# Rows of the later experts brought by indirect DMA and turned, in place of one-hot products

## The chip, the cores and the metric

The kernel runs on one core of a Trainium2 chip. The metric is the device time of one execution in microseconds (us), as the median of several runs. Engines are named as in the profile: PE is TensorE, PEld its weight load, DVE is VectorE, ACT is ScalarE, POOL is GpSimd, SP is SyncE, which issues most of the DMAs.

## What is computed

A trunk of two layers on 256 tokens of 1024 channels, all in float32. The first layer is attention of two kinds and a dense feed-forward; the second is banded attention and an expert feed-forward. Only the last of these is touched by the change. Cut to what matters:

```python
def moe_swiglu(h, w_router, we_gate, we_up, we_down):      # h is x after its RMS norm
    t = h.reshape(b * s, d)                                # 256 x 1024
    logits = (t @ w_router).astype(F32)                    # 8 experts
    top_val, top_idx = lax.top_k(logits, TOP_K)            # 2 a token
    gates = jax.nn.softmax(top_val, axis=-1)
    combine = jnp.einsum('tk,tke->te', gates, jax.nn.one_hot(top_idx, N_EXPERTS, dtype=F32))
    y = jnp.zeros_like(t)
    for e in range(N_EXPERTS):                             # each 1024 -> 3584 -> 1024
        y = y + combine[:, e:e + 1].astype(t.dtype) * swiglu(t, we_gate[e], we_up[e], we_down[e])
    return y.reshape(b, s, d)
```

The weights of the eight experts are 352 MB (8 x 3 x 1024 x 3584 x 4 bytes), and each is read once.

## The kernel before

The expert stage begins at about 430 us of the profiled span and lasts to its end. The kernel computes an expert only for the tokens that chose it. It gives each expert 96 slots (`CAP`), 64 of them main slots and 32 overflow slots; the overflow products stand in a branch (`arm`, L1118) that runs only if the expert has more than 64 tokens. A later pass for experts with more than 96 tokens (L1426) stands behind another branch.

**Slots.** The router's choice gives for each token and expert `sel` (1 or 0) and `pos` (its slot). `dispatch(e)` (L900) makes on DVE two one-hot matrices of 256 tokens by 96 slots: `dx`, tile `dispx`, whose ones are scaled by the token's reciprocal RMS `rx`, and `dt`, tile `disp`, unscaled. Each takes two DVE instructions (L906), one for each 128 tokens.

**Gather.** `Rows.gather` (L917) multiplies x, token-major in SBUF, with `dx` on PE: for each block of 128 channels two products of 128 tokens. The result is the expert's input, channel-major, in a room `xg` (two rooms, by the expert's parity; one is a part of the tile `oTh`). DVE reads it from PSUM and multiplies it by the norm's gain (L923). This is done twice for an expert, for four channel blocks each.

**Chunks.** The 3584 hidden channels of each expert are cut into chunks, and the experts go in pairs. `order` (L808 on) gives 18 chunks: for experts 0 and 1 five, for 2 and 3 and for 4 and 5 four each (1536 of the even expert, 1536 of the odd one, 2048 even, 2048 odd), for 6 and 7 five. For each chunk `experts` (L1147) does the gate columns, the up columns (`cols`, L1195) and then the down rows of the chunk before (`down`, L1162). `cols` and `down` take weights in batches of up to four pieces: first the main products of the batch, then, in the branch, the overflow products.

**Pieces.** Weights come in pieces of at most 1 MB by SP's queue. `pieces_of` (L843) lists them in the order in which they are consumed, and `Pieces.more` (L858) issues as many as a batch has used. A ring of some twenty buffers (tags `raw`, `rawb`, `w`, `hTl`, and for one use each `yx` and `oTl`) holds them; a DMA waits on SP until the last reader of its buffer is done.

**End of an expert.** After the last up columns of an expert, `turn` (L1038) transposes `dt` of the main slots by products with the identity, and, after the down rows of the chunk before, `turn_over` (L1044) those of the overflow slots. These transposed one-hots later put the expert's output rows back to their tokens (`add`, `add_over`, `finish`).

**Order.** `in_order` (L184) keeps PE, ACT and DVE each in the order of the program text, so a step that waits holds all that is behind it on its engine. In this order, where the next chunk is the first one of an expert, `nxt.room()` makes the two one-hots of that expert right behind `x.turn()`, then come the down rows, `turn_over` and the two gathers:

```python
                nxt = found[to.e] if to and to.i == 0 else None
                if nxt:
                    nxt.room()
                if i:
                    down(i - 1, i)
                if q.last:
                    x.turn_over()
                if nxt:
                    nxt.rows.gather(range(0, 4))
                    nxt.rows.gather(range(4, 8))
```

PSUM has four banks (`spin`, `banks`) in rotation for gate and up columns, gathers, transposes and sums, two for the down sums of the main slots (`za`) and two for those of the overflow slots (`zb`).

Of the kernel before, what the change touches and what calls it, by code (L numbers as in the profile page):

```python
# [47 lines left out]
def kernel(ctx: ExitStack, tc: tile.TileContext, A: dict, out: bass.AP):  # L48
# [772 lines left out]

    def piece():
        return raw_tile().rearrange("p a b -> p (a b)")
# [18 lines left out]

    def pieces_of():  # L843
# [6 lines left out]
        for q, before in zip(chunks, [None] + chunks):  # L850
            for w in (eg[q.e], eu[q.e]):
                for k in range(0, KB, max(1, 2048 // q.n)):
                    yield cols_piece(w, q.c0, q.n, k)
            if before:
                yield from downs(before)
# [19 lines left out]
    with ExitStack() as ph:  # L875
# [6 lines left out]
        both = act.tile([P, 2, P], BF, name="both", tag="disp", bufs=2)  # L882
# [7 lines left out]
        for k in range(GROUPS):  # L890
            nc.gpsimd.memset(quarter[k * OV:(k + 1) * OV, k % 2:k % 2 + 1], 1.0)
        comb = act.tile([P, T, NE], F32, name="comb")
# [7 lines left out]
        def dispatch(e):  # L900

            dt = act.tile([P, T, CAP], F32, name="disp", bufs=2)
            dx = act.tile([P, T, CAP], F32, name="dispx")
            for o, value in ((dx, selx), (dt, sel)):
                for t in range(T):
                    nc.vector.tensor_scalar(o[:, t], slots, pos[:, t, e:e + 1], value[:, t, e:e + 1], op0=OP.is_equal,  # L906
                                            op1=OP.mult)
            return dt, dx

        class Rows:  # L910


            def __init__(self, e, room):
                self.dt, self.dx = dispatch(e)
                self.xg = room

            def gather(self, kbs):  # L917
                o = banks(1)[0].rearrange("p (b s) -> p b s", b=4)
                for b, kb in enumerate(kbs):
                    for t in range(T):  # L920
                        mm(o[:, b, 0:CAP], x[:, t, kb * P:(kb + 1) * P], self.dx[:, t], t == 0, t == T - 1)
                k = kbs[0]
                nc.vector.tensor_tensor(self.xg[:, k:k + 4], o[:, :, 0:CAP],  # L923
                                        cst[:, C_GF1 + k:C_GF1 + k + 4, None].to_broadcast([P, 4, CAP]), op=OP.mult)
# [17 lines left out]
        def main_cols(o, rows, tiles, n, kb0):  # L942

            for b, (c, w) in zip(o, parts(n)):
                for kb, r in enumerate(rows_in(tiles), kb0):
                    for k in range(2):
                        at = k * n // 2 + c
                        mm(b[k * MAIN:(k + 1) * MAIN, 0:w], rows.xg[:, kb, 0:MAIN], r[:, at:at + w],
                           kb == 0, kb == KB - 1)

        def over_cols(o, rows, tiles, n, kb0):
            w = over_width(n)
            for kb, r in enumerate(rows_in(tiles), kb0):
                for k in range(GROUPS):
# [4 lines left out]
                    mm(to, rows.xg[:, kb, MAIN:CAP], cols, kb == 0, kb == KB - 1)  # L959
# [62 lines left out]
        class Expert:  # L1022


            def __init__(self, e, rv):
                self.e, self.rv = e, rv
                self.y, self.yo = ys[e % 2], yos[e % 2]

            def room(self):
                self.rows = Rows(self.e, rooms[self.e % 2])  # L1030

            def turned(self, o, n, ss):

                for t in range(T):
                    for k in range(0, P, n):
                        mm(o[k:k + n, t], self.rows.dt[:, t, ss], ident, True, True)
# [93 lines left out]
        def spans(n):  # L1130

            return [(i, min(4, n - i)) for i in range(0, n, 4)]

# [13 lines left out]
        def experts(rows, feed, first, rvs):  # L1147
# [3 lines left out]
            found[0].rows = rows  # L1151
# [43 lines left out]
            def cols(x, main, over, n, mid=None, end=None):  # L1195
# [3 lines left out]
                for p, (i0, m) in enumerate(cuts):  # L1199
                    tiles = feed.take(m)  # L1200
                    main_cols(main, x.rows, tiles, n, i0 * nk)
# [278 lines left out]
```

## Time and profile before

| | us |
|---|---|
| median of 3 runs (1320.77 to 1322.87) | 1321.46 |
| profiled execution, its own time | 1321.63 |
| span of that execution's instructions | 1319.9 |
| PE busy | 1274.8 |
| DVE busy | 378.9 |
| ACT busy | 322.2 |
| POOL busy | 11.0 |

The profiled execution is one run; its span goes from the first instruction to the end of the last, and 1.7 us of its time lie outside. The granted clock of TensorE was 0.996 over the span. PE's busy time counts matmuls from start to a modelled end, so that products that overlap in the array look like one busy stretch. The stage of the experts is the last two thirds of the span. A group of rows in the timeline has the start, the duration from the first to the last of its instructions, the engine, line, operation, tiles as out<-in, shape, the count, and in brackets the idle time before it and what ended it.

### The profile page before, as it was taken

What the parts mean: (1) busy time and instruction counts of PE and PEld (TensorE: products, weight loads), DVE (VectorE), ACT (ScalarE), POOL (GpSimd) and SP (SyncE); (2) the same over time, 40 slices, a digit from 0 to 9 for tenths busy, and PEclk for the clock granted to TensorE, in tenths of its full rate; (3) what the DMA queues carried; (4) which work ended last, traced back from release to release, by engine and by line L of the source; (5) the groups of instructions that cost most, each with busy time, mean ns of one, the idle gap of its engine ahead of it and who ended that gap; (6) DMA issues with size and microseconds to landing.
All of it is one profiled execution on the core that took longest, in us unless ns stands there. A gap on an engine that the chain in (4) does not pass through costs nothing. (4 is left out here: it accounts for less than half of the span.)

```text
span 1319.9 us, 19560 instructions
## 1 busy us (share of the span) xinstructions
PE 1274.8 (97%) x7887; PEld 698.6 (53%) x7887; DVE 378.9 (29%) x723; ACT 322.2 (24%) x593; POOL 11.0 (1%) x38
## 2 busy tenths in 40 slices
PE   9999999999999989999999999999999999999995
PEld 6777888888777743342444343344433344333442
DVE  7965554446788510000111000111100001110011
ACT  7665544446566400100100000000000010000000
POOL 0000000000000000000000000000000000000000
PEclk9999999999999999999999999999999999999998
DMA  9623555555454989999998999999999999999961
GB/s 348 233 68 127 189 178 175 190 191 182 162 161 148 395 322 404 423 421 420 390 420 368 420 422 424 418 420 409 423 422 421 421 418 422 422 422 419 415 262 38
DMA packets 90254, 426.70 MB, mean 323 GB/s; under 512 B 7568, under 2 KB 10256, under 8 KB 59408
## 3 DMA queue, kind: packets, MB, share of 16 engines
q1 hardware_dynamic: 89056, 422.80, 80.2%
q0 software_dynamic: 640, 2.10, 0.7%
q8 instruction: 85, 1.39, 0.4%
q14 instruction: 41, 0.34, 0.1%
q10 hardware_dynamic: 432, 0.07, 0.0%
HBM read 423.89 MB, written 1.05 MB: 322 GB/s over the span
## 5 line engine op out<-in xcount | busy, mean ns | idle before, releaser
L59 PE MATMUL mm<-w,hTh 128*128 128x512 f32 x736 | 240.1, 400 | 0.4 <-DVE w L143 0.4
L143 DVE TENSOR_TENSOR w<-raw,w 128x1024 fp32r<-128x1024 f32 (+1 forms) x127 | 153.9, 1214 | 90.8 <-ACT w L142 90.4
L59 PEld LDWEIGHTS mm<-w,hTh 128*128 128x128 f32 x736 | 137.7, 188 | 32.5 <-issue 1.3
L142 ACT ACTIVATE w<-raw 128x1024 fp32r<-128x1024 f32 (+1 forms) x127 | 133.5, 1053 | 86.5 <-PE mm L59 51.2
L59 PE MATMUL mm<-w,hTl 128*128 128x512 f32 x368 | 146.5, 398 | 0.0
L1143 DVE TENSOR_TENSOR a<-tr,a 128x512 f32<-128x512 f32 (+1 forms) x16 | 9.7, 609 | 254.7 <-PE tr L59 249.9
L59 PE MATMUL za<-raw,hTh 128*64 128x512 f32 x360 | 81.5, 595 | 0.7 <-PEq L1123 0.7
L59 PEld LDWEIGHTS mm<-w,hTl 128*128 128x128 f32 x368 | 69.4, 188 | 14.8
L1143 DVE TENSOR_TENSOR a<-mm,a 128x512 f32<-128x512 f32 (+1 forms) x16 | 10.3, 642 | 227.7 <-PE mm L59 197.9
L59 PE MATMUL mm<-w,oTh 128*64 128x512 f32 (+2 forms) x224 | 57.3, 522 | 0.9 <-PEq L1123 0.8
L59 PE MATMUL za<-rawb,hTh 128*64 128x512 f32 x256 | 57.6, 593 | 0.4 <-DMA w<-in_od_we_gate 0.2
L59 PE MATMUL mm<-raw,xg 128*64 128x512 f32 (+4 forms) x356 | 56.5, 544 | 0.3 <-PEq L1123 0.3
L59 PE MATMUL tr<-rawb,xg 128*32 128x128 f32 (+4 forms) x484 | 54.9, 450 | 1.8 <-DVEq L1123 1.5
L59 PE MATMUL tr<-raw,xg 128*64 128x512 f32 (+4 forms) x364 | 55.5, 537 | 0.0
L59 PE MATMUL mm<-raw,oTh 128*64 128x512 f32 (+1 forms) x240 | 48.9, 535 | 3.4 <-DVE comb L1399 1.4
L59 PEld LDWEIGHTS za<-raw,hTh 128*64 128x64 f32 x360 | 26.5, 137 | 46.8 <-issue 44.8
L59 PE MATMUL za<-w,hTh 128*64 128x512 f32 x224 | 50.5, 595 | 0.4 <-PEq L1123 0.4
L1145 ACT ACTIVATE a<-mm 128x512 f32<-128x512 f32 (+1 forms) x18 | 10.1, 562 | 161.4 <-PE mm L59 161.3
L59 PE MATMUL mm<-rawb,oTh 128*64 128x512 f32 (+1 forms) x216 | 45.5, 559 | 2.1 <-ACTq L1123 1.2
L59 PE MATMUL tr<-w,xg 128*64 128x512 f32 (+4 forms) x296 | 46.8, 528 | 0.3 <-PEq L1123 0.3
L59 PE MATMUL mm<-rawb,xg 128*64 128x512 f32 (+4 forms) x300 | 46.6, 545 | 0.3 <-DMA w<-in_od_we_down 0.3
L969 ACT ACTIVATE hTh<-tr 128x512 f32<-128x512 f32 (+1 forms) x18 | 9.0, 536 | 149.3 <-PE tr L968 149.3
(340 smaller groups left out, 1466.7 us busy)
## 6 DMA issues: line engine op xcount, KB each, us to landing
raw<-in_od_we_down SPq DMA_DIRECT2D x45, 1024.0 KB, 15.7
rawb<-in_od_we_down SPq DMA_DIRECT2D x32, 1024.0 KB, 15.5
raw<-in_od_we_gate SPq DMA_DIRECT2D x29, 1024.0 KB, 15.4
raw<-in_od_we_up SPq DMA_DIRECT2D x28, 1024.0 KB, 17.8
w<-in_od_we_down SPq DMA_DIRECT2D x28, 1024.0 KB, 16.6
rawb<-in_od_we_up SPq DMA_DIRECT2D x27, 1024.0 KB, 19.4
rawb<-in_od_we_gate SPq DMA_DIRECT2D x23, 1024.0 KB, 14.1
w<-in_od_we_gate SPq DMA_DIRECT2D x20, 1024.0 KB, 15.0
```

The source lines that it names most:

```text
L59: nc.tensor.matmul(o, lhsT, rhs, start=start, stop=stop, skip_group_check=True)
L142: nc.scalar.activation(hi[:, s], r[:, s], AF.Copy)
L143: nc.vector.tensor_tensor(lo[:, s], r[:, s], hi[:, s].bitcast(F32), op=OP.subtract)
L969: nc.scalar.activation(dst[:, b:b + n], pt[:, 0:n], AF.Copy)
L1143: nc.vector.tensor_tensor(a[:, c:c + w], o[:, 0:w], a[:, c:c + w], op=OP.mult)
L1145: nc.scalar.activation(a[:, c:c + w], o[:, 0:w], AF.Silu)
```

## The change

For experts 2 to 7 the one-hot gather goes. Instead:

- `store` writes x (1 MB), when its last residual is added, to a memory tensor `stored`, by two DMAs of SP's queue. They are issued behind the first two pieces that wait for a buffer and ahead of those of the `w`, `hTl` and `yx` buffers.
- `lists_in`, behind the up columns of chunk 1, makes the unscaled one-hots of experts 2 to 7 (12 instructions of DVE, into the tile `oTl`), multiplies them on PE with a two-column table `token` (token number and `rx`), and copies the result into one list of token numbers and one of scales for each expert (12 DVE copies of 96 x 1). The ring gets the `oTl` buffer only after that.
- `brought` issues on POOL, for both experts of a pair, an indirect DMA of 96 rows of 4 KB from `stored` into one ring buffer. It stands in the list of pieces ahead of the last batch of up columns of chunks 4, 8 and 12, which are the chunks before the pairs 2/3, 4/5 and 6/7.
- `scale_rows`, ahead of that last batch, multiplies these rows by the scales on ACT (two instructions of 96 x 1024).
- `rows_from`, behind that batch, transposes them on PE: eight transposes of 96 x 128 for each expert, four into one bank, and DVE multiplies each bank by the gain as before (four instructions for the pair).
- The unscaled one-hot of an expert (`hot`) is no longer made ahead. `turn` makes it, for all experts but the first, just before its products read it. Its tile has one buffer instead of two.
- `turn_over` moves from behind the down rows to behind the gate columns of the next chunk.

Experts 0 and 1 are still gathered by products. The diff, cut to its core:

```diff
+    def brought(es):
+        def load():
+            r = piece()
+            for j, e in enumerate(es):
+                nc.gpsimd.indirect_dma_start(out=r[0:CAP, j * D:(j + 1) * D], out_offset=None, in_=stored[:, :],
+                                             in_offset=bass.IndirectOffsetOnAxis(ap=lists[e][0][0:CAP, 0:1], axis=0))
+            return r
+        return load
...
+            nk = max(1, 2048 // q.n)
+            for up, w in enumerate((eg[q.e], eu[q.e])):
+                for k in range(0, KB, nk):
+                    if up and starts(i) and k == spans(KB // nk)[-1][0] * nk:
+                        yield brought(starts(i))
                     yield cols_piece(w, q.c0, q.n, k)
...
+        def list_of(es, hots):
+            o = banks(1)[0][:, 0:2 * len(es)].rearrange("p (e v) -> p e v", v=2)
+            for j, d in enumerate(hots):
+                for t in range(T):
+                    mm(o[0:CAP, j], d[:, t], token[:, t], t == 0, t == T - 1)
+            for j, e in enumerate(es):
+                nc.vector.tensor_copy(lists[e][0][0:CAP], o[0:CAP, j, 0:1])
+                nc.vector.tensor_copy(lists[e][1][0:CAP], o[0:CAP, j, 1:2])
...
-            def room(self):
-                self.rows = Rows(self.e, rooms[self.e % 2])
+            def rows_from(self, r):
+                for k in (0, 4):
+                    pt = banks(1)[0].rearrange("p (b s) -> p b s", b=4)
+                    for b in range(4):
+                        nc.tensor.transpose(pt[:, b, 0:CAP], r[0:CAP, (k + b) * P:(k + b + 1) * P], ident[0:CAP, 0:CAP])
+                    scaled(self.xg, pt, k)
...
             def turn(self):
                 self.dT = total[2][:, self.e % 2]
+                self.dt = self.dt or hot(self.e)
...
+                if late:
+                    late.pop().turn_over()
                 if before:
                     before.add(0)
...
+                def scale_rows():
+                    rows.extend(feed.take(1))
+                    for j, e in enumerate(es):
+                        r = rows[0][0:CAP, j * D:(j + 1) * D]
+                        nc.scalar.activation(r, r, AF.Copy, scale=lists[e][1][0:CAP])
+
-                cols(x, u, uo, n, None, (up, up_over))
+                cols(x, u, uo, n, None, (up, up_over), scale_rows if es else None)
+                for j, e in enumerate(es):
+                    found[e].rows_from(rows[0][:, j * D:(j + 1) * D])
+                if es:
+                    feed.more(1)
                 if before:
                     before.add(1)
+                if i == 1 and lists_in:
+                    lists_in()
                 if q.last:
                     if not total:
                         total.extend(sums())
                     x.turn()
-                to = chunks[i + 1] if i + 1 < len(chunks) else None
-                nxt = found[to.e] if to and to.i == 0 else None
-                if nxt:
-                    nxt.room()
+                    late.append(x)
+                one = i + 1 < len(chunks) and chunks[i + 1].e == 1 and not chunks[i + 1].i
+                if one:
+                    gather_first(1, [0])
                 if i:
                     down(i - 1, i)
-                if q.last:
-                    x.turn_over()
-                if nxt:
-                    nxt.rows.gather(range(0, 4))
-                    nxt.rows.gather(range(4, 8))
+                if one:
+                    gather_first(1, [1])
+            late.pop().turn_over()
             down(len(chunks) - 1)
...
+        def store(h):
+            s = slice(h * 512, h * 512 + 512)
+            nc.sync.dma_start(stored[:, s].rearrange("(t p) c -> p t c", p=P), x[:, :, s])
...
         pieces.more(2)
+        for h in range(2):
+            store(h)
...
+        nc.vector.tensor_copy(token[:, :, 1], norm.rx)
...
+        def lists_in():
+            hots = wide.tile([P, 2, 1024], F32, name="oTl").rearrange("p a b -> p (a b)")
+            hots = hots[:, 0:(NE - 2) * T * CAP].rearrange("p (e t s) -> p e t s", e=NE - 2, t=T)
+            for e in range(2, NE):
+                one_hot(hots[:, e - 2], e, sel)
+            list_of(range(2, NE), [hots[:, e] for e in range(NE - 2)])
+            ring.appendleft((wide, "oTl"))
+            pieces.more(1)
```

## Rows read from the trace of the kernel before

**Rows 1.** The page, its first part: busy time of each engine.
```profile
PE 1274.8 (97%) x7887; PEld 698.6 (53%) x7887; DVE 378.9 (29%) x723; ACT 322.2 (24%) x593; POOL 11.0 (1%) x38
```
**Rows 2.** Busy us by stretch: PE, PEld, DVE, ACT, POOL; clock, DMA share, GB/s.
```profile
460.00:500.00 40.00, 36.14 (x223) 19.52 (x223) 5.54 (x17) 2.77 (x6) 0.00 (x0) 1.00 0.85 336
...
1000.00:1100.00 100.00, 96.84 (x626) 38.17 (x618) 9.73 (x20) 6.28 (x12) 0.00 (x0) 1.00 1.01 420
```
**Rows 3.** Waits from 500 us on: who, for whom, total us, times, longest.
```profile
DVE a L1143 <- PE tr L59: 249.9, 13, 53.2
...
PEld za L59 <- DMA rawb<-in_od_we_gate: 2.3, 7, 0.6
```
**Rows 4.** Waits of the DMA queue of SP from 400 us on.
```profile
SPq L831 <- PEq L1123: 110.4, 29, 8.0
```
**Rows 5.** Timeline, 1176 to 1214 us: one piece, its issue and its first use.
```profile
1178.84 0.38 SPq L839 DMA_DIRECT2D hTl<-in_od_we_down  x1
...
1211.52 1.92 PE L59 MATMUL za<-hTl,hTh 128*64 128x512 f32 x8
```
**Rows 6.** The tile hTl, 1170 to 1230 us: its two DMAs, issue to landing.
```profile
DMA to landing us min/median/max: 16.2/18.1/20.1
```
**Rows 7.** Timeline, 1068 to 1073 us, PE: gather of an even expert (6).
```profile
1068.49 0.65 PE L59 MATMUL mm<-ident,disp 128*32 128x128 f32 x16 [1.57 <-DVEq L1123]
...
1069.06 3.81 PE L59 MATMUL tr<-dispx,x 128*128 128x96 f32 x32
...
1072.80 5.38 PE L59 MATMUL mm<-w,oTh 128*64 128x512 f32 x32
```
**Rows 8.** Timeline, 1121 to 1126 us, PE: gather of an odd expert (7).
```profile
1121.39 3.78 PE L59 MATMUL tr<-dispx,x 128*128 128x96 f32 x32 [0.46 <-DVE yx L1055]
...
1125.10 1.08 PE L59 MATMUL mm<-hTl,xg 128*64 128x512 f32 x4
```
**Rows 9.** Timeline, 1273 us, PE: gate columns straight behind an expert's last down rows.
```profile
1273.16 2.16 PE L59 MATMUL tr<-rawb,xg 128*64 128x256 f32 x18 [1.48 <-DVEq L1123]
```
**Rows 10.** Timeline, 453 and 486 to 489 us: the place of the lists, and narrow products.
```profile
453.44 1.05 PE L59 MATMUL zb<-ident,a 16*128 16x8 f32 x8
...
486.88 0.69 DVE L1143 TENSOR_TENSOR a<-mm,a 128x512 f32<-128x512 f32 x1 [15.98 <-PEq L1123]
...
486.92 3.65 PE L59 MATMUL za<-raw,hTh 128*64 128x512 f32 x16 [0.16 <-PEq L1123]
...
487.73 0.57 DVE L906 TENSOR_SCALAR dispx<-slots,pos,selx 128x96 f32<-128x96 f32 x2
...
488.21 0.57 DVE L906 TENSOR_SCALAR disp<-slots,pos,sel 128x96 f32<-128x96 f32 x2
```
**Rows 11.** Timeline, 1050 to 1124 us: end of chunk 12; eight transposes; a gain multiply.
```profile
1050.17 0.66 PE L59 MATMUL mm<-ident,disp 128*64 128x128 f32 x8
...
1050.36 0.69 DVE L1249 TENSOR_TENSOR aos<-mm,aos 128x512 f32<-128x512 f32 x1 [2.88 <-PE mm L59]
...
1057.62 1.22 PE L968 MATMUL tr<-ident,a 128*128 128x128 f32 x8
...
1123.42 0.56 DVE L923 TENSOR_TENSOR xg<-tr,cst 128x384 f32<-128x384 f32 x1 [0.20 <-PE tr L59]
```
**Rows 12.** Timeline, 989 us: end of chunk 11, the last of an even expert.
```profile
989.48 0.69 DVE L1143 TENSOR_TENSOR a<-mm,a 128x512 f32<-128x512 f32 x1 [2.75 <-PEq L1123]
...
989.52 0.66 PE L59 MATMUL tr<-ident,disp 128*64 128x128 f32 x8
```
**Rows 13.** Timeline, 1285 us: end of chunk 17, the last one of all.
```profile
1285.46 0.66 PE L59 MATMUL tr<-ident,disp 128*64 128x128 f32 x8
...
1285.57 1.41 DVE L1055 SCALAR_TENSOR_TENSOR yx<-mm,comb,yx 128x512 f32<-128x512 f32 x2 [0.27 <-PE mm L59]
```
**Rows 14.** DMA issues: the only transfers of POOL's queue; KB each, median us to landing.
```profile
rb<-in_rel POOLq DMA_DIRECT2D x8, 256.0 KB, 4.0
```
**Rows 15.** Timeline, 445 us: the last residual of x.
```profile
445.72 1.28 DVE L341 TENSOR_TENSOR x<-x,za 128x512 f32<-128x512 f32 x2
```

More of the change, by code (lines that the diff above doesn't have):

```diff
@@ L820, with starts, spans @@
     chunks = order()
+    def starts(i):
+        q = chunks[i + 1] if i + 1 < len(chunks) else None
+        return [] if not q or q.i or q.e % 2 else [q.e, q.e + 1]
+    def spans(n):
+        return [(i, min(4, n - i)) for i in range(0, n, 4)]
     def piece():
@@ L898, with one_hot @@
         aos = act.tile([P, 512], F32, name="aos")
[L900 to L904, printed above, removed]
-                for t in range(T):
[L906 to L924, printed above, removed]
+        def one_hot(o, e, value):
+            for t in range(T):
+                nc.vector.tensor_scalar(o[:, t], slots, pos[:, t, e:e + 1], value[:, t, e:e + 1], op0=OP.is_equal,
+                                        op1=OP.mult)
+            return o
@@ new lines, in hot, with scaled, gather @@
+        def hot(e):
+            return one_hot(act.tile([P, T, CAP], F32, name="disp"), e, sel)
+        def scaled(xg, o, k):
+            nc.vector.tensor_tensor(xg[:, k:k + 4], o[:, :, 0:CAP],
+                                    cst[:, C_GF1 + k:C_GF1 + k + 4, None].to_broadcast([P, 4, CAP]), op=OP.mult)
+        def gather(dx, xg, k):
+            o = banks(1)[0].rearrange("p (b s) -> p b s", b=4)
+            for b in range(4):
+                for t in range(T):
+                    mm(o[:, b, 0:CAP], x[:, t, (k + b) * P:(k + b + 1) * P], dx[:, t], t == 0, t == T - 1)
+            scaled(xg, o, k)
@@ L1145, in activate, with experts @@
                     nc.scalar.activation(a[:, c:c + w], o[:, 0:w], AF.Silu)
-        def experts(rows, feed, first, rvs):
+        def experts(dt, feed, first, rvs, lists_in=None):
             found = [Expert(e, rvs[e] if rvs else None) for e in range(NE)]
-            found[0].rows = rows
+            found[0].dt, late = dt, []
             ao, turned, ready = aos, [], []
@@ L1297 @@
         residual(acc, 0)
+        lists = [[act.tile([P, 1], U32, name=f"to{e}"), act.tile([P, 1], F32, name=f"rs{e}")] for e in range(NE)]
+        stored = ph.enter_context(tc.tile_pool(name="rows", bufs=1, space=bass.MemoryType.DRAM)).tile(
+            [S, D], F32, name="stored")
+        def store(h):
+            s = slice(h * 512, h * 512 + 512)
+            nc.sync.dma_start(stored[:, s].rearrange("(t p) c -> p t c", p=P), x[:, :, s])
         norm = Norm(C_GF1)
@@ L1379 @@
         spin = [bank("tr") for _ in range(2)]
-        rows = Rows(0, rooms[0])
+        dx = one_hot(act.tile([P, T, CAP], F32, name="dispx"), 0, selx)
+        dt0 = hot(0)
         nc.vector.tensor_copy(count, pp[:, T])
@@ L1391 @@
         gate(1, 3)
-        rows.gather(range(0, 4))
+        gather(dx, rooms[0], 0)
         nc.scalar.activation(sh[:, 1], g[1], AF.Silu, scale=norm.rx[:, 1:2])
-        rows.gather(range(4, 8))
+        gather(dx, rooms[0], 4)
         nc.vector.tensor_scalar(gt[:, :, 2:3], gt[:, :, 1:2], 1.0, None, op0=OP.add)
@@ L1430 @@
                 with in_order():
-                    rows = Rows(0, rooms[0])
-                    rows.gather(range(0, 4))
-                    rows.gather(range(4, 8))
+                    gather_first(0)
+                    for e in range(2, NE):
+                        list_of([e], [hot(e)])
                     pieces = Pieces(pieces_of())
                     pieces.more(len(ring))
-                    experts(rows, pieces, None, None)
+                    experts(hot(0), pieces, None, None)
 _BIG = ("ev_w_in", "ev_w_out", "ev_w_gate", "ev_w_up", "ev_w_down", "od_w_qkv", "od_w_out",
```

53 lines of the change are left out of this document (32 added, 21 removed).

## The prediction, made before the changed kernel was run

> **What bounds the kernel now.** I began with the page's busy times: PE is busy for 97% of the span, DVE for 29%, POOL for 1% [rows 1]. Then the busy times by stretch: in the experts' stage PE is busy for 96.84 of 100 us, but the DMA engines are full as well, at 420 GB/s with a share of 1.01 [rows 2]. So two engines look like the bound, and the waits have to tell them apart. In the waits from 500 us on, DVE waits for PE's products for hundreds of us, and the largest wait of PE's weight loads for a landed piece is 2.3 us in seven parts of at most 0.6 [rows 3]. SP's queue, on the other side, waits for PE to give buffers back, 110.4 us in its longest entry [rows 4]. One piece followed by hand says the same: issued at 1178.84 us, first read at 1211.52 [rows 5]; its tile's two transfers in that stretch took at most 20.1 us to land [rows 6], so it lay ready for at least 12.6 us (1211.52 - 1178.84 - 20.1). PE is therefore the bound, with the DMA stream only a little faster: a microsecond on PE's path is a microsecond of the kernel, and DMA bytes cost nothing until they have used up these 12.6 us. I take that piece because it stands behind a run of batches without overflow products, where PE runs through pieces fastest.
>
> **What goes.** An odd expert's gather starts at 1121.39 us and its first gate product at 1125.10, 3.7 us [rows 8]; an even one's lies between 1069.06 and 1072.80, 3.74 us [rows 7]. Six gathers go: 6 x 3.74 = 22.4 us of PE. The waits just ahead of them (0.46 us for a sum, 1.57 us for DVE's split in the row of `turn_over`) stay: they are for PSUM banks, and where gate columns follow an expert's last down rows directly today, PE waits 1.48 us all the same [rows 9]. If these waits went with the odd gathers, up to 0.46 us more would be won for each, and I allow 25 us as the other end. DVE's scaled one-hots and gain multiplies of these experts stood beside PE's work; four gain multiplies a pair come back.
>
> **What the lists add.** They stand where PE goes from the up columns of chunk 1 to down rows, at 486.92 us. DVE ends its multiply at 487.57 and makes a pair of one-hot instructions every 0.48 us from 487.73 on [rows 10]. Six pairs: the last starts at 487.73 + 5 x 0.48 = 490.13 and ends at 490.70. PE's products of one expert (four records at 1.05 / 8 = 0.13 us, from the narrow products [rows 10]) end 0.5 us behind it, at about 491.3, and only then do the down rows begin: 4.4 us, with no cover. The lower end is 24 x 0.13 = 3.1 us, were the one-hots ready; the upper 6.4, if the next products also waited for the twelve small copies at about 0.17 us (estimated from the smallest spacing of short DVE instructions, 487.73 - 487.57). The `oTl` piece is loaded later for it, in a stretch where the stream has room [rows 2], so I take that at nothing.
>
> **What the turned rows add, three times.** At the end of chunk 12, PE goes from overflow products to `turn` at 1050.17 us, and DVE's last multiply runs from 1050.36 to 1051.05 [rows 11]. Now 16 transposes come between: 16 x 1.22 / 8 = 2.4 us. But DVE ends later than PE: four gain multiplies of 0.56 us behind 1051.05 end at 1053.3, and the one-hot that `turn` now makes for itself stands behind them, 0.57 us, to 1053.9. `turn`'s products begin at about 1054.0: 3.8 us a pair, 11.4 in all. Lower end 2.4 each (DVE free in time); upper 5.9, if PE and DVE took turns on each bank: 4 x (0.61 + 0.56) + 0.57 + 0.69. ACT's scaling has no row of its shape; by DVE's 0.69 us for 512 columns, two times 1024 are some 2.8 us, and it stands ahead of a batch of up columns (a batch's main products alone take 5.4 us [rows 7]), which covers it; uncovered it would be 2.8 us a pair.
>
> **The one-hot made late.** At the end of chunks 7, 11 and 15 `turn` starts at 989.52 us; DVE's multiply ends at 990.17, and the one-hot behind it at about 990.9 [rows 12] (0.16 us between, as at 487.57). PE waits 1.5 us more, 4.5 in all; ends 1.3 and 2.0 each. At the end of chunk 17 two sums of DVE end at 1286.98, the one-hot at 1287.6, and `turn` starts then instead of at 1285.46 [rows 13]: 2.2 us, ends 1.5 and 2.8. Chunk 3 has its one-hot.
>
> **The moved `turn_over`.** Its products are the same 0.65 us. Its branch was entered while PE waited for DVE [rows 7]; behind gate columns nothing covers that. At a branch PE has a gap of 0.16 us [rows 10]; for one at its entry and one at its end I take 0.3 us for three experts, 0.9 in all; ends 0 and 2.
>
> **The queues.** SP is moved past two stores. x is final at 447.0 us [rows 15] and SP's next issues come behind, so SP does not wait; 1 MB takes 1.05 / 0.42 = 2.5 us of the stream, in a stretch that has 15% of 40 us free [rows 2]. POOL's queue has nothing behind the gathers. Each brings 0.79 MB for a pair, 1.9 us at 420 GB/s; POOL's only other transfers land in 4.0 us for 256 KB [rows 14], and these are issued when a ring buffer comes free, as far ahead of their use as other pieces (32.7 us in [rows 5]). Their buffer is given back some 4 us late, and SP waits in order for it; since a piece lands 16 to 20 us after its issue [rows 6], several are still under way then. All told 2.5 + 3 x 1.9 = 8.2 us of stream, less than 12.6. I take it at nothing.
>
> **The sum.** 4.4 + 11.4 + 4.5 + 2.2 + 0.9 - 22.4 = +1.0 us. The ends are 3.1 + 7.2 + 3.9 + 1.5 + 0 - 25 = -9.3 and 6.4 + 17.7 + 6.0 + 2.8 + 2 - 22.4 = +12.5. Against the profiled execution: span 1319.9 + 1.0, with 1.7 outside it, 1322.6. That execution lies 0.2 above the median of the runs, 1321.46; on the median 1322.5, ends 1312.2 and 1334.0. Change in the work is large; what is taken from PE comes back as waits of PE for DVE.
>
> **The rivals.** *The waits for DVE don't appear* (1309.4 us). If `turn`'s one-hot does not stand last on DVE, and the lists find theirs made, PE pays bare work: 3.1 + 3 x 2.4 - 22.4 = -12.1. For it: DVE is idle for up to 53.2 us ahead of these multiplies [rows 3]. Against it: idle ahead does not help, since program order puts the one-hot behind them.
>
> *The stream becomes the bound* (slower, about 1329.5 us). Place: the pieces behind each gather. It decides from 12.6 us of added stream on, which is 3.4 us a pair in place of 1.9. At the rate of POOL's lone transfers, 4.0 us for 256 KB, a pair would take 12; half of that, 6, gives 2.5 + 18 - 12.6 = +7.9. For it: the DMA share of 1.01 [rows 2]. Against it: the waits [rows 3] and the piece that lay ready [rows 5, 6]. [...]
>
> *The rows come too late, so that the change does not do what it says* (above 1335): the first gather would have to take tens of us; ACT would then hold on its scaling, and PE behind it.
>
> **How the numbers follow.** Forecast (PE's path, the sum with its ends) 0.62, no waits for DVE 0.19, the stream 0.16, late rows 0.03. The forecast's own range is 1317 to 1327. The range of 8 in 10 goes from 1313 to 1332, which takes in most of the ends and the stream, and leaves out the full gain and the late rows. A measurement of this kernel can tell about 0.2%, 2.6 us, from no change. Of the forecast's 0.62, 0.34 lie within that, 0.10 below and 0.18 above; the gain adds 0.19 to faster; the stream 0.14 to slower and 0.02 to same, the late rows 0.03 to slower: 0.29, 0.36, 0.35.
>
> **What would show it.** In the changed kernel: no products of `dispx` from chunk 2 on; 16 transposes at the ends of chunks 4, 8, 12, and behind them PE idle for about 1.4 us until a one-hot of DVE (L906's successor); idle of 1.5 us at the ends of chunks 7, 11, 15 and of 2.2 at 17; PE at half pace for 4.4 us at 487 us; from each gather's old place 3.7 us less. PE waits for landed pieces stay under a few us, else the stream rules. Wrong would be the forecast if DVE's one-hots stand earlier, or if a gather's landing shows up in a wait of ACT or PE.

## The result, and the profile of the changed kernel

The changed kernel takes 1331.28 us (median of 4 runs, 1329.70 to 1333.57), the kernel before 1322.16 beside it: a ratio of 1.0071, 95% interval 1.0053 to 1.0090. It is slower by 9.1 us. The likeliest forecast, no change (1322.5, its own range 1317 to 1327), was wrong. The range of 8 in 10, 1313 to 1332, holds the measured time, just under its end, and the time is near that of the rival in which the stream becomes the bound (1329.5), which had a chance of 0.16. The profiled execution is the longest of the four: span 1331.8, 11.9 us more than before, with a mean granted clock of 0.990 against 0.992 in the other three.

Rows of the changed kernel that answer to [rows 1, 2]: the page's line for PE; then busy us by stretch (PE, PEld, DVE, ACT, POOL; clock, DMA share, GB/s), and last the third stretch in the kernel before.

```profile
PE 1271.2 (95%) x7767; PEld 688.9 (52%) x7767; DVE 379.1 (28%) x736; ACT 328.6 (25%) x599; POOL 16.9 (1%) x45
```
```profile
460.00:500.00 40.00, 34.70 (x190) 18.13 (x189) 8.39 (x42) 3.56 (x7) 0.00 (x0) 0.91 0.87 339
1000.00:1100.00 100.00, 94.40 (x630) 36.96 (x626) 7.21 (x13) 9.55 (x16) 0.00 (x0) 1.00 1.01 412
1200.00:1280.00 80.00, 73.72 (x522) 28.76 (x520) 3.07 (x6) 3.43 (x7) 0.00 (x0) 0.96 1.01 406
```
```profile
1200.00:1280.00 80.00, 77.29 (x626) 33.41 (x624) 3.78 (x6) 4.69 (x10) 0.00 (x0) 1.00 0.95 388
```

PE has less work, 3.6 us, in a span that is 11.9 us longer: from 1000 to 1100 us it is busy for 94.40 us in place of 96.84, with the DMA share at 1.01 in both. And the granted clock, 1.00 in these stretches before, is 0.91 and 0.96 in two of them.

What PE waits for, from 500 us on (answers to [rows 3]; total us, times, longest):

```profile
PE tr L59 <- DVE disp L928: 6.2, 4, 1.7
...
PEld mm L59 <- DMA raw<-in_od_we_up: 5.3, 4, 2.3
...
PEld mm L59 <- DMA w<-in_od_we_up: 2.8, 4, 2.0
PE mm L59 <- DMA raw<-in_od_we_up: 2.7, 2, 1.4
```

The waits for one-hots were forecast. The waits for pieces were not: in these rows PE's matmuls wait 7.2 us in all for a landed piece, before 0.5. (One of 1.53 us, at 1076.83, stands where PE waits 1.53 us for DVE in the other two pairs; without it 5.7 us are left.) Where that happens shows in the timeline of PE, 1198 to 1222 us, the up columns of chunk 15 and the down rows behind them:

```profile
1202.13 1.08 PE L59 MATMUL mm<-w,oTh 128*64 128x512 f32 x4 [1.09 <-DMA w<-in_od_we_up]
...
1209.99 1.08 PE L59 MATMUL mm<-raw,oTh 128*64 128x512 f32 x4 [1.25 <-DMA raw<-in_od_we_up]
1212.48 1.97 PE L59 MATMUL mm<-raw,oTh 128*64 128x512 f32 x4 [1.41 <-DMA raw<-in_od_we_up]
1214.24 1.92 PE L59 MATMUL tr<-w,oTh 128*64 128x512 f32 x4
...
1221.44 0.66 PE L59 MATMUL mm<-ident,disp 128*64 128x128 f32 x8 [1.44 <-DVE disp L928]
1221.90 1.92 PE L59 MATMUL za<-raw,hTh 128*64 128x512 f32 x8
```

Piece after piece comes too late, and from 1212 us on four products take 1.92 to 1.97 us in place of 1.08: from 1212 to 1218 us the granted clock is 0.50, in the kernel before 1.00. The last row is the first use of the piece of [rows 5], 10.4 us later than before. Its issue from SP's queue, and its time to landing (last number):

```profile
1194.68 0.33 SPq L848 DMA_DIRECT2D raw<-in_od_we_down  x1
```
```profile
raw<-in_od_we_down SPq DMA_DIRECT2D x1, 1024.0 KB, 20.2
```

It landed at 1214.9; before it was issued at 1178.84 and took 16.2, the least of [rows 6]: 1195.0. The stream runs 19.8 us behind here, more than the 12.6 us that the prediction allowed. (The pieces of the up columns just ahead, for which PE waits, are as late: the last of them landed at 1192.5 before, and here PE waits for it until 1212.48.)

Last, one gather: POOL's two issues, and the DMA lines from 500 to 620 us in 40 slices of 3 us (busy tenths of the 16 engines; GB/s), with the queues' packets, MB and shares.

```profile
575.31 1.00 POOL L857 DMA_INDIRECT rawb<-stored,to  x1 [156.73 <-DVEq L1172]
576.62 0.93 POOL L857 DMA_INDIRECT rawb<-stored,to  x1 [0.31 <-issue]
```
```profile
DMA  9923999999999999999999999999999999999999
GB/s 382 410 87 68 415 423 426 410 426 426 410 423 418 421 412 418 426 421 418 418 415 421 421 415 421 423 367 310 313 378 418 423 426 404 418 423 418 423 421 415
...
q0 software_dynamic: 224, 0.79, 2.2%
```

In the four slices from 578 us the engines stay busy and yet move 367, 310, 313 and 378 GB/s in place of 420. That is (53 + 110 + 107 + 42) x 3 us = 0.94 MB not moved, and 0.79 MB of what was moved are rows: the weights are thrown back by 1.73 MB, 4.1 us. The prediction had 1.9.

### The profile page after: what moved, and what is told of

It reads as the page before. It is cut to its first block, busy times and chain, and to the rows that moved or that the text cites. A ratio compares the mean times of both kernels' runs of the same rounds, so it can differ in the third digit from the quotient of the medians.

```text
span 1331.8 us, 19367 instructions
## 1 busy us (share of the span) xinstructions
PE 1271.2 (95%) x7767; PEld 688.9 (52%) x7767; DVE 379.1 (28%) x736; ACT 328.6 (25%) x599; POOL 16.9 (1%) x45
## 5 line engine op out<-in xcount | busy, mean ns | idle before, releaser
L59 PE MATMUL za<-rawb,hTh 128*64 128x512 f32 x296 | 66.8, 594 | 0.4 <-PEq L1172 0.4
L59 PE MATMUL mm<-raw,xg 128*32 128x512 f32 (+5 forms) x460 | 58.6, 498 | 0.8 <-issue 0.4
L59 PE MATMUL tr<-raw,xg 128*64 128x512 f32 (+3 forms) x316 | 53.6, 531 | 0.0
L59 PE MATMUL mm<-w,oTh 128*64 128x512 f32 (+2 forms) x184 | 48.4, 511 | 2.2 <-PEq L1172 1.1
L59 PE MATMUL tr<-w,xg 128*64 128x512 f32 (+3 forms) x272 | 49.0, 561 | 1.4 <-DMA w<-in_od_we_gate 1.0
L59 PE MATMUL tr<-rawb,xg 128*64 128x512 f32 (+3 forms) x296 | 47.8, 541 | 2.2 <-DVEq L1172 1.5
L59 PE MATMUL mm<-w,xg 128*32 128x512 f32 (+4 forms) x392 | 49.5, 509 | 0.0
L255 DVE TENSOR_TENSOR oTl<-za,oTl 128x512 fp32r<-128x512 f32 x8 | 5.5, 692 | 140.8 <-ACT oTl L254 71.6
L1190 ACT ACTIVATE a<-tr 128x512 f32<-128x512 f32 (+1 forms) x17 | 9.3, 547 | 146.1 <-PE tr L59 146.1
L1012 ACT ACTIVATE hTh<-mm 128x512 f32<-128x512 f32 (+1 forms) x17 | 9.3, 557 | 140.6 <-PE mm L1011 122.3
```

The source lines that it names most:

```text
L59: nc.tensor.matmul(o, lhsT, rhs, start=start, stop=stop, skip_group_check=True)
L255: nc.vector.tensor_tensor(lo, src, hi.bitcast(F32), op=OP.subtract)
L1012: nc.scalar.activation(dst[:, b:b + n], pt[:, 0:n], AF.Copy)
L1190: nc.scalar.activation(a[:, c:c + w], o[:, 0:w], AF.Silu)
```

## The experiments

All are edits of the changed kernel. For each the table has the median, the ratio to the kernel before in the same runs, the lag of the piece of [rows 5] (its issue plus its time to landing, less 1195.0), and where PE starts the down rows that read it, less 1211.5. Lag and PE come from the one profiled execution of each kernel. Two landings are missing in the records; there the last piece of the same four is taken.

| kernel | us | ratio, 95% interval | lag | PE |
|---|---|---|---|---|
| changed | 1331.3 | 1.0071 (1.0053 to 1.0090) | +19.8 | +10.4 |
| no gather traffic | 1326.1 | 1.0028 (1.0019 to 1.0038) | +9.0 | -0.5 |
| lists' one-hots early | 1325.1 | 1.0018 (1.0009 to 1.0028) | +14.1 | +1.6 |
| own one-hot early | 1325.9 | 1.0028 (1.0016 to 1.0041) | +18.9 | +5.2 |
| both early | 1323.3 | 1.0005 (0.9996 to 1.0014) | +14.6 | +0.9 |
| both early, no gather traffic | 1312.2 | 0.9922 (0.9907 to 0.9937) | +4.8 | -7.4 |
| plain 96 x 4 KB, of stored | 1337.4 | 1.0119 (1.0103 to 1.0135) | +23.6 | +11.0 |
| plain 96 x 4 KB, of weights | 1337.8 | 1.0113 (1.0097 to 1.0128) | +25.1 | +14.0 |
| plain 96 x 8 KB, of weights | 1337.7 | 1.0120 (1.0104 to 1.0135) | +25.7 | +13.2 |
| plain 128 x 4 KB, of weights | 1326.4 | 1.0030 (1.0020 to 1.0040) | +12.8 | +1.9 |
| indirect 128 rows | 1325.9 | 1.0027 (1.0017 to 1.0037) | +15.5 | +4.6 |
| both early, 128 rows | 1320.1 | 0.9980 (0.9971 to 0.9989) | +11.2 | -1.0 |
| both early, 128 rows, two pairs | 1315.3 | 0.9949 (0.9935 to 0.9963) | +6.4 | -7.2 |

Two theories stood at the start. STREAM: the gathers' transfers cost the stream more than their bytes, and PE waits for the weights behind them. PE: the stops of PE itself, for lists, turned rows and late one-hots, and the lower clock behind them.

**Without the gathers' traffic.**
```diff
-                nc.gpsimd.indirect_dma_start(out=r[0:CAP, j * D:(j + 1) * D], out_offset=None, in_=stored[:, :],
-                                             in_offset=bass.IndirectOffsetOnAxis(ap=lists[e][0][0:CAP, 0:1], axis=0))
+                nc.gpsimd.memset(r[0:CAP, j * D:(j + 1) * D], 0.5)
```


> The changed kernel, but POOL writes 0.5 into the gathered rows with a memset in place of each indirect DMA: the reading of rows from stored is left out, and with it the right input of experts 2 to 7; everything else on PE, DVE and the queues is as changed. If the gathers' transfers are what makes the kernel slower (theory STREAM: some 4 to 5 us of the stream a pair, so that pieces land some 20 us later by 1100 us and PE waits for them), three gathers of 4.1 to 5.1 us go: landings from chunk 11 on are some 13 us earlier, PE's waits for pieces at 1011, 1101 and 1198 us go, and the time is about 1322 us (1320 to 1325). If PE's own gaps and its clock are the cause (theory PE: lists, rows and late one-hots delay the ring and drop the granted clock at 492, 639 and 1212 us), the time stays at 1329 to 1331.


Measured 1326.1: 5.2 of the 9.1 us go, neither theory's number, but only 1 us above that of STREAM. The lag at 1212 us falls from 19.8 to 9.0, so three gathers are 10.8 us of it; the other 9 us come from elsewhere. The memset also costs something of its own: at the ends of chunks 7 and 11 it runs beside DVE's one-hot, which takes 1.16 us at chunk 7 in place of 0.57, and PE waits 2.2 us in place of 1.44 there. PE's own path is the later one in this kernel, so some 1.5 us of its time are likely to be the memset's.

```profile
780.65 1.84 POOL L857 MEMSET rawb<- 96x1024 f32 x2 [205.61 <-PEq L1171]
781.45 1.16 DVE L927 TENSOR_SCALAR disp<-slots,pos,sel 128x96 f32<-128x96 f32 x2
```

**The lists' one-hots early.**
```diff
                 part = ao[:, 0:ow]
+                if i == 1 and lists_in:
+                    hots_in()
...
-        def lists_in():
+        def hots_in():
...
+            hots_made.append(hots)
+        def lists_in():
+            hots = hots_made.pop()
```


> The changed kernel with DVE's one-hots of the six experts' lists made ahead of the gate columns of chunk 1 instead of behind its up columns, so that PE's list products find them ready. Nothing is left out. Theory PE: the 4.3 us at 487 us fall to about 3.1 or less, PE stays busy, the granted clock does not fall to half at 492 to 498 us, which cost 3 us, and the landings from 523 us on come some 4 us earlier: the time falls by 4 to 7 us, to about 1324 to 1327. Theory STREAM: the ring frees earlier by some 4 us as well, but what the gathers take from 715 us on is not changed; of the 4 us no more than 1 to 3 arrive at the end, 1328 to 1330.


Measured 1325.1, the number of PE. PE between 487 and 493 us, and the clock of that stretch:

```profile
487.23 2.17 PE L59 MATMUL tr<-token,oTl 128*96 128x2 f32 x24 [0.31 <-PEq L1172]
489.33 3.65 PE L59 MATMUL za<-raw,hTh 128*64 128x512 f32 x16
```
```profile
460.00:500.00 40.00, 35.85 (x229) 20.30 (x230) 8.80 (x39) 2.94 (x6) 0.00 (x0) 1.00 0.87 341
```

The wait for the one-hots is gone, and with it the low clock behind it: the 16 products take 3.65 us in place of 6.63, and the granted clock of the stretch is 1.00 in place of 0.91. The lag at 1212 us falls by 5.7 us, with all three gathers in place: what PE loses at 487 us comes back as lateness of pieces 700 us on. The stretch behind the stop shows how, first in the changed kernel, then here:

```profile
500.00:520.00 20.00, 20.00 (x162) 10.06 (x164) 1.12 (x2) 1.35 (x4) 0.00 (x0) 1.00 0.79 310
500.00:520.00 20.00, 20.00 (x164) 8.03 (x164) 0.00 (x0) 1.47 (x3) 0.00 (x0) 1.00 1.01 413
```

Behind the stop the stream runs partly empty (share 0.79), for want of buffers that PE gives back late (SP's queue waits 24.4 us for PE from 485 to 515 us); with early lists it stays full (1.01). (413 - 310) x 20 us are 2.1 MB, 4.9 us at 420 GB/s.

**Each expert's own one-hot early**, behind the gate columns of its last chunk.
```diff
                 if late:
                     late.pop().turn_over()
+                if q.last:
+                    x.dt = x.dt or hot(x.e)
```


> The changed kernel with the next expert's one-hot made behind the gate columns of an expert's last chunk, ahead of its up columns, instead of last on DVE behind the gains: turn no longer waits for it. Nothing is left out. By PE's path alone three times 1.4 us at the ends of chunks 4, 8 and 12, three times 1.3 us at 7, 11 and 15 and 1.8 us at 17 fall away or shrink to what DVE's gains still cost: 5 to 9 us less in PE's gaps. Theory PE: the time falls by 5 to 8 us, to about 1323 to 1326. Theory STREAM: what PE wins from chunk 11 on it waits again for pieces, and only 1 to 4 us show, 1327 to 1330.


Measured 1325.9, at the upper end of PE's 1323 to 1326. `turn` no longer waits: PE's gap at the end of chunk 12 is 1.5 us more than before in place of 3.0, at 7, 11, 15 and 17 next to none. But the lag stays at 18.9: unlike the stop at 487 us, these stops hardly count on the stream. In the changed kernel SP's queue waits 24.4 us from 485 to 515 us, all of it for PE, but from 975 to 1005 us, around the late one-hot of chunk 11, it waits 20.7 us for earlier transfers to land and not at all for PE. And PE's matmuls wait 11.3 us for pieces in place of 7.2. Three single edits take away 5.2, 6.2 and 5.4 us of 9.1, more than there is, so the losses overlap.

**Both early.** The two diffs above together.


> Both edits to the order of DVE's one-hots: the lists' made ahead of chunk 1's gate columns, and each expert's own made ahead of the up columns of its last chunk. Nothing is left out. Alone they took 6.2 and 5.4 us off the change. By PE's gaps the two add up, 11.6 us, to about 1319.5. By the stream they don't: in the kernel with early lists a piece lands 14.1 us behind the kernel before at 1212 us, and PE's late place there is that lag less 12.6 us; the early one-hots take about 1 us more off the lag, so that PE stands at about +0.5 us there, and with 0 to 1 us behind it the time is 1322 to 1324, that of the kernel before.


Measured 1323.3, as expected from the lag. Only 1.8 us come on top of the better of the two, because PE at 1212 us stands where the pieces let it.

**Both early, without the gathers' traffic.** The two diffs, and the memset of the first.


> Both edits to the order of DVE's one-hots, and POOL's memset of 0.5 in place of the indirect DMAs (the reading of rows from stored is left out, so experts 2 to 7 get wrong input). Without the gathers' 11 us the pieces at 1212 us land only 2 to 4 us behind the kernel before, so PE's own path sets the time: lists +2.3, turned rows 3 x 1.5, moved turn_over 3 x 0.85, gathers -24.4, the late one-hots about 0, together some -15, of which 12 to 15 can show: 1308 to 1311 us. If the stream costs stay although no rows come (the buffer that the rows hold is one less for pieces), it stays above 1316.


Measured 1312.2, 1 us above the expected: most of PE's gain shows as soon as the rows don't travel. The same three gathers cost 5.2 us (or 6.7 without what the memset seems to cost there) while PE stops as well, and 11.1 us (1323.3 - 1312.2) when it doesn't. What was left was why they are so dear.

**Plain transfers of the same size.**
```diff
-                nc.gpsimd.indirect_dma_start(out=r[0:CAP, j * D:(j + 1) * D], out_offset=None, in_=stored[:, :],
-                                             in_offset=bass.IndirectOffsetOnAxis(ap=lists[e][0][0:CAP, 0:1], axis=0))
+                nc.sync.dma_start(r[0:CAP, j * D:(j + 1) * D], stored[0:CAP, :])
```


> The changed kernel, but each indirect DMA is replaced by a plain DMA from SP's queue of the same size (rows 0 to 95 of stored, 384 KB): the choice of rows is left out, so experts 2 to 7 get wrong rows; bytes and everything behind them are as changed. If bytes alone count (theory BYTES, the prediction's 1.9 us a pair), the stream carries as much as with the gathers and the time is that of the change, about 1331. If the indirect form costs more than its bytes (theory STREAM: 4 to 5 us a pair), the stream wins back 2 to 3 us a pair, 6 to 9 us in all, and the time is about 1323 to 1326, between the kernel without gathers and the change. By theory PE it stays at 1329 to 1331 as well, but then the kernel without gathers does too.


Measured 1337.4, slower than with indirect ones and 6 us above what either theory gave. It is not the indirect form.

**The same, read from other memory.**
```diff
-                nc.sync.dma_start(r[0:CAP, j * D:(j + 1) * D], stored[0:CAP, :])
+                nc.sync.dma_start(r[0:CAP, j * D:(j + 1) * D], ed[e][0:CAP, :])
```


> As the kernel with plain DMAs of 96 rows from SP's queue, but the 384 KB come from rows 0 to 95 of the expert's down weights instead of stored: shape, bytes, queue and place in SBUF are the same, only the memory that is read differs (the choice of rows is left out, experts 2 to 7 get wrong rows). That kernel measured 1337.4 us, and its weight packets ran slower while the rows came (DMA at 246 to 266 GB/s with the engines at nine tenths or more). If it is stored's memory that is slow under these reads (theory SOURCE), the pair costs about its 1.9 us here, GB/s stays near 420, landings at 1212 us are some 7 to 11 us earlier than with stored, and the time is about 1327 to 1329, as without gathers. If it is the shape (96 partitions of 4 KB) or the mere added bytes (theory SHAPE), it is 1335 to 1339 again.


Measured 1337.8, as SHAPE has it: the memory that is read is not the cause. GB/s from 500 to 620 us:

```profile
GB/s 377 311 0 229 429 412 412 421 431 421 415 421 423 421 415 412 421 421 415 421 421 421 423 407 421 423 421 421 418 410 415 217 235 378 418 423 418 423 423 407
```

The dip (217, 235) is deeper than that of the indirect form.

**96 partitions or 4 KB.** Two edits of the last kernel, one for each.
```diff
-                nc.sync.dma_start(r[0:CAP, j * D:(j + 1) * D], ed[e][0:CAP, :])
+                nc.sync.dma_start(r[0:P, j * D:(j + 1) * D], ed[e][0:P, :])
```


> As the kernel with plain DMAs from the down weights (1337.8 us, landings 24.3 us behind the kernel before at 1036 us, 5.7, 7 and 7.6 us lost at the three pairs), but 128 rows to 128 partitions in place of 96 to 96: 1.05 MB a pair, a third more bytes, still in packets of 4 KB (which rows a gather would pick is left out, experts 2 to 7 get wrong rows). If it is the 96 partitions that make the rows dear (theory PARTITIONS), a pair costs its bytes, 1.05 / 0.42 = 2.5 us, GB/s stays near 420 beside it, landings come 8 to 13 us earlier from 1036 us on, and the time is 1328 to 1330. If it is the packets of 4 KB beside those of 8 KB (theory PACKETS) or any second small transfer (theory ISSUE), a third more bytes make it no faster: 1337 to 1342.


```diff
-            for j, e in enumerate(es):
-                nc.sync.dma_start(r[0:CAP, j * D:(j + 1) * D], ed[e][0:CAP, :])
+            nc.sync.dma_start(r[0:CAP, 0:2 * D], ed[es[0]][0:2 * CAP, :].rearrange("(p j) c -> p (j c)", j=2))
```


> As the kernel with plain DMAs from the down weights, but a pair's 0.79 MB come in one transfer of 96 partitions by 8 KB (two rows behind each other) in place of two transfers of 96 by 4 KB (experts 2 to 7 get wrong rows). If the 96 partitions make the rows dear (theory PARTITIONS), it stays at 1335 to 1339. If it is the packets of 4 KB (theory PACKETS), or that there are two transfers (theory ISSUE), a pair costs its 1.9 us and the time is 1327 to 1330.


Measured 1326.4 with 128 partitions, a little under the forecast, and 1337.7 with 96 by 8 KB, both on the side of PARTITIONS. GB/s from 500 to 620 us, first 128 x 4 KB, then 96 x 8 KB:

```profile
GB/s 415 262 55 382 423 429 393 423 421 421 426 410 426 418 412 423 426 415 415 412 426 426 412 415 426 418 423 415 412 418 404 431 404 423 426 412 421 426 407 426
```
```profile
GB/s 399 292 0 246 426 407 412 429 426 412 418 426 415 423 421 407 423 421 415 423 415 421 431 399 426 423 415 426 407 418 423 235 208 374 412 423 426 412 423 415
```

In the place where the second line falls to 235 and 208, the first stays above 400 with a third more bytes.

**128 rows in the changed kernel.**
```diff
-                nc.gpsimd.indirect_dma_start(out=r[0:CAP, j * D:(j + 1) * D], out_offset=None, in_=stored[:, :],
-                                             in_offset=bass.IndirectOffsetOnAxis(ap=lists[e][0][0:CAP, 0:1], axis=0))
+                nc.gpsimd.indirect_dma_start(out=r[0:P, j * D:(j + 1) * D], out_offset=None, in_=stored[:, :],
+                                             in_offset=bass.IndirectOffsetOnAxis(ap=lists[e][0][0:P, 0:1], axis=0))
...
+        for e in range(2, NE):
+            nc.gpsimd.memset(lists[e][0], 0)
```


> The changed kernel with indirect DMAs of 128 rows in place of 96 and nothing else; the list's other 32 places are row 0. Nothing of the computation is left out. Under theory PARTITIONS a pair costs about 3 us of the stream in place of 4.3, the pieces at 1212 us land 16 us behind the kernel before in place of 20, PE stands 3.4 us late there instead of 7 to 10, and with the 1.8 us at chunk 17 the time is 1325 to 1329. If the gain of 3.2 us from 96 to 128 rows seen behind the early one-hots was something else, it stays at 1330 to 1333.


Measured 1325.9, as PARTITIONS has it: 5.4 us are won by bringing more. GB/s and POOL's queue from 500 to 620 us:

```profile
GB/s 366 421 71 71 426 418 418 407 426 415 423 423 410 429 412 418 429 410 426 415 410 429 412 423 423 412 419 422 419 411 407 423 429 399 431 423 412 426 410 418
...
q0 software_dynamic: 288, 1.05, 2.2%
```

No dip from 575 us on (412, 419, 422, 419), and 1.05 MB take the same 2.2% of the engines' time as 0.79 MB before.

**Both early, 128 rows.** The three diffs above together.


> The kernel with both edits to DVE's one-hots (1323.3 us, PE at +0.9 us at 1212 us, where pieces land 14.6 us later than before), with indirect DMAs of 128 rows to 128 partitions in place of 96; the list's other 32 places are row 0, and nothing reads what they bring. Nothing of the computation is left out. Under theory PARTITIONS a pair costs 2.5 us in place of 4.2 to 4.5, the lag at 1212 us falls by 5 to 6 us, and PE stands 5 us earlier there: 1317 to 1319 us, faster than the kernel before by 0.3%. Under theory PACKETS a third more bytes cost a third more, 1.4 us a pair: 1325 to 1328.


Measured 1320.1, 1 us above what PARTITIONS gave and well under PACKETS, and the first with the whole computation that is faster than the kernel before. PE's matmuls still wait 9.7 us for pieces.

**Two pairs of three.** As the kernel with both early and 128 rows, but the last pair goes back to one-hot products, which cost PE and spare the stream; lists are made for four experts.
```diff
-        return [] if not q or q.i or q.e % 2 else [q.e, q.e + 1]
+        return [] if not q or q.i or q.e % 2 or q.e == NE - 2 else [q.e, q.e + 1]
...
-                one = i + 1 < len(chunks) and chunks[i + 1].e == 1 and not chunks[i + 1].i
+                one = chunks[i + 1].e if i + 1 < len(chunks) and not chunks[i + 1].i else 0
+                one = one if one in (1, NE - 2, NE - 1) else 0
```


> Both edits to DVE's one-hots and indirect DMAs of 128 rows, but for the pairs of experts 2, 3 and 4, 5 alone; experts 6 and 7 get their rows by one-hot products as in the kernel before. Nothing is left out. PE pays 2 x 3.8 us of products again and saves the turned rows and turn_over of that pair, some +5.6 us on its own path; the stream saves one pair's 3 us, so that the lag at 1212 us falls from 11.2 to about 8 us. If the stream sets the end (theory STREAM), PE may stand 4.5 us earlier than in the kernel before at 1212 us, where it stood 1.0 earlier with three pairs: 1315 to 1318 us. If PE's path sets it, the time rises to 1323 to 1326.


Measured 1315.3, as STREAM has it: more work for PE, and 4.8 us less time. Faster than the kernel before by 0.5%, and the fastest with the whole computation. PE from 1000 to 1100 and from 1200 to 1280 us:

```profile
1000.00:1100.00 100.00, 96.67 (x626) 38.49 (x622) 9.35 (x18) 7.15 (x14) 0.00 (x0) 1.00 1.01 418
...
1200.00:1280.00 80.00, 77.21 (x704) 35.20 (x702) 7.30 (x13) 5.07 (x11) 0.00 (x0) 1.00 1.00 398
```

Both stretches are back at PE's share and at the clock of the kernel before.

## Where the prediction held and where it failed, point by point

**PE's path: right.** Read off against DVE's last multiply at each place, as the prediction did. The changed kernel's rows, first the lists, then the ends of chunks 12, 11 and 17, then the place of an even expert's gather and a moved `turn_over` (timeline of DVE and PE):

```profile
487.98 0.69 DVE L1188 TENSOR_TENSOR a<-mm,a 128x512 f32<-128x512 f32 x1 [15.98 <-PEq L1172]
...
489.30 3.11 PE L59 MATMUL tr<-token,oTl 128*96 128x2 f32 x24 [1.44 <-DVE oTl L928]
492.34 6.63 PE L59 MATMUL za<-raw,hTh 128*64 128x512 f32 x16
...
1055.69 0.69 DVE L1298 TENSOR_TENSOR aos<-mm,aos 128x512 f32<-128x512 f32 x1 [2.88 <-PE mm L59]
1056.30 1.01 DVE L937 TENSOR_TENSOR oTh<-tr,cst 128x384 f32<-128x384 f32 x2
...
1058.53 0.68 PE L59 MATMUL tr<-ident,disp 128*64 128x128 f32 x8 [1.50 <-DVE disp L928]
...
992.27 0.69 DVE L1188 TENSOR_TENSOR a<-mm,a 128x512 f32<-128x512 f32 x1 [2.75 <-PEq L1172]
...
993.60 0.66 PE L59 MATMUL tr<-ident,disp 128*64 128x128 f32 x8 [1.44 <-DVE disp L928]
...
1295.69 0.75 DVE L1104 SCALAR_TENSOR_TENSOR yx<-mm,comb,yx 128x512 f32<-128x512 f32 x1 [0.27 <-PE tr L59]
...
1297.39 0.68 PE L59 MATMUL tr<-ident,disp 128*64 128x128 f32 x8 [1.74 <-DVE disp L928]
...
866.96 1.08 PE L59 MATMUL mm<-hTl,oTh 128*64 128x512 f32 x4 [1.53 <-DVEq L1172]
...
1088.17 0.64 PE L59 MATMUL mm<-ident,disp 128*32 128x128 f32 x16 [0.43 <-ACTq L1172]
```

- Lists: 492.34 - 487.98 = 4.36, before 0.04 [rows 10]: 4.3, forecast 4.4.
- Turned rows: 1058.53 - 1055.69 = 2.84, before -0.19 [rows 11]: 3.0; the same at chunks 4 and 8, 9.1 in all, forecast 11.4. Two gain multiplies in a row take 1.01 and not 1.12.
- One-hot late: 1.33, before 0.04 [rows 12]: 1.3, three times, 3.9; forecast 4.5. Chunk 17: 1.70, before -0.11 [rows 13]: 1.8, forecast 2.2.
- `turn_over` behind the gate columns adds 0.84 us, and 0.57 of it (1069.06 - 1068.49) went from its old place [rows 7]: 0.3 more, three times, 0.8; forecast 0.9.
- The gathers gone: 3.8 us for each expert, 22.7; forecast 22.4. The waits ahead of them stayed, as forecast: 1.53 in place of 1.57.

Together 4.3 + 9.1 + 3.9 + 1.8 + 0.8 - 22.7 = -2.8, forecast +1.0. So the forecast time would have been about right, had PE's path alone set it. The kernel without the gathers' traffic, in which PE's path is the later, is the nearest test: 1326.1, inside the forecast's own range, with the memset's 1.5 us in it and a granted clock of 0.96 from 460 to 500 us (before 1.00).

**The queues: here it failed.** "I take it at nothing" rested on 8.2 us of added stream against 12.6 us of lead. The 12.6 came out near the mark, in part by luck: they take one transfer's issue and another's time to landing. The piece itself lay ready for 16.5 us (1211.52 - 1195.0), and the last piece of the up columns just ahead, for which PE waits now, for 13.9 (landed at 1192.5, first read at 1206.4). In the table PE stands within 1.7 us of the lag less 12.6 in eleven kernels of thirteen: 23.6 - 12.6 = 11.0 (11.0 measured), 25.7: 13.1 (13.2), 14.1: 1.5 (1.6), 11.2: -1.4 (-1.0). The two others are the changed kernel, 7.2 (10.4), whose clock falls to 0.50 there, and the one without the gathers' traffic alone, -3.6 (-0.5), where PE's own path is the later. What was set against it was wrong in two terms:
- A pair of gathers was sized by its bytes, 1.9 us; it costs 4.1. Three are 10.8 us in the lag (19.8 - 9.0), not 5.7. The form of the transfer, 96 partitions, does it: with 128 rows, a third more bytes, three are 6.5 (15.5 - 9.0).
- PE's stop at the lists was counted once, on PE's path. It counts on the stream as well: while the ring is full, SP waits for PE to give buffers back [rows 4], and at 487 us the stop was long enough for the stream to run partly empty behind it (share 0.79). With early lists alone the lag at 1212 us is 5.7 us smaller (0.9 of it scatter ahead of the stage, below). What the prediction took at nothing there, the later load of the `oTl` piece, is one piece, not the whole queue behind it. The later stops hardly count twice: without the late one-hots the lag is 18.9 in place of 19.8, and with early lists 14.6 in place of 14.1.

The 3.3 us that are left of the lag (19.8 - 10.8 - 5.7) no run assigns. The store of x, sized at 2.5 us of stream, left little: with early lists the piece that the kernel before issues at 471 us lands 5.5 us later than there, the one that it issues at 527 us 0.9 later.

**The clock: not in the sum.** The 16 products at 492.34 took 6.63 us, before 3.65 [rows 10]; ahead of them PE had waited 1.44 us and run 24 narrow products. That is 3.0 us, 1.7 more stand at 639 us and 3.0 at 1212. The granted clock is 0.50 from 492 to 498 us, 0.54 from 639 to 642 and 0.50 from 1212 to 1218, in the kernel before 1.00 in all three; over the longer stretches (460 to 500, 600 to 700, 1200 to 1280 us) that leaves 0.91, 0.98 and 0.96. Together with PE's 5.7 us of waits for pieces, the span adds up: -2.8 + 7.7 + 5.7 + 1.1 that PE was late ahead of the stage = 11.7, measured 11.9. (The 1.1 is scatter: kernels that are alike up to there stand at -0.1 to 1.5.) Which of the falls come back in which execution isn't settled: with early lists the clock at 487 us was 1.00 in three kernels and 0.96 in two.

**The rivals.** No waits for DVE: those waits are there. The stream: its time, 1329.5, came near the measured 1331.3 in part by luck, for it sized a pair at 6 us, too high, and left out the stop at the lists. PE stands at the later of its own path and about the lag less 12.6 us, so bytes rule from there on alone, and PE's stop at 487 us counts besides, since it feeds the lag.

## What to carry to other kernels

Where the DMA share is 1.01 and PE is the bound by a lead of a few microseconds, keep an account of the lead: add what a change brings onto the stream and the stops of PE behind which the stream runs empty, and compare the sum with the lead at its smallest place. Count a transfer by how it is spread over partitions, not by its bytes alone: here a pair of 128 rows cost about its bytes (2.2 us of lag for 2.5 us of bytes at 420 GB/s), one of 96 about twice its bytes (4.1 us for 1.9). And when an edit pays on one engine and costs on the other, try doing it only as often as the lead allows: two pairs of three beat both three and none here.

## What the runs showed that was not expected

Beside the stream of weights (DMA share 1.01) the transfers to 96 partitions cost more than those to 128 with a third more bytes (1331.3 us against 1325.9 for indirect rows, 1337.8 against 1326.4 for plain ones): GB/s fell to 310 for indirect rows and to 208 to 242 for plain ones, with the engines busy throughout, and stayed at 404 or more while rows of 128 came. Neither the source, nor the indirect or plain form, nor 4 or 8 KB a partition took the dip away. In the changed kernel's records of single packets the weights slow as well as the rows: from 580 to 587 us their packets of 8 KB take 425 to 453 ns, by the median of each microsecond, in place of 313 before the rows come, and the rows' packets of 4 KB 206 to 231 in place of the 161 of the first ones. No run tells whether it is the number 96 or the places 0 to 95 in SBUF: no other number and no other place than from 0 on was tried. And why 96 cost more than 128, and plain transfers more than indirect ones (1337.4 us against 1331.3), no trace here shows: both stay open.
